# Attention scores on the keys that count: 256 neighbours and 128 of the residue class, in plain fp32 on 64x32 pieces

## The chip, the cores and the metric

The kernel runs on one core of one Trainium2 chip. The metric is the device time of one execution in microseconds; the kernel before takes 543.53 us as the median of three runs (543.14 to 543.93). The core has five engines that run their own instruction streams in order of program and meet through semaphores: TensorE (PE in the profile, with PEld for its weight loads), VectorE (DVE), ScalarE (ACT), GpSimd (POOL) and SyncE (SP, which here only issues transfers).

## The reference

One layer of an encoder for 512 positions of 1024 features, cut to the attention group:

```python
DILATED_PATTERNS = ((128, 1), (512, 4), (2048, 16))
for window, dil in DILATED_PATTERNS:
    half = window // (2 * dil)
    offs = jnp.arange(-half, half + 1) * dil          # 129 offsets, step dil
    bias = rel_bias[t5_bucket(offs)].T
...
for offs, bias in pats:                               # for each block of 128 queries
    kpos = pos[:, None] + offs[None, :]
    valid = (kpos >= 0) & (kpos < S)
    logits = einsum('bqhd,bqjhd->bhqj', qb, k[:, clip(kpos)]) * scale + bias
    logits = where(valid, logits, NEG_INF)
    lse = logsumexp(logits); p = exp(logits - lse)
    outs.append(einsum('bhqj,bqjhd->bqhd', p, v[:, clip(kpos)])); lses.append(lse)
o = sum(softmax(lses) * outs)                          # over the three patterns
```

There are 8 heads of 64 features. Combined by their softmax denominators, the three patterns are one softmax in which a key at distance `rel` counts as often as patterns contain it. All distances up to 64 occur; beyond 64 only multiples of 4 (up to 256) and of 16 do. Around the attention stand: an RMSNorm and one combined input projection (x_r, gate, q, k, v), a recurrent group (convolution, gates, a forward and a backward scan), an output projection of both groups (each after its own RMSNorm) with a residual, an MLP with squared ReLU, and a last RMSNorm.

## The kernel before, in words

Almost all matrix work is fp32 split into a rounded high part and a low part (`hi`, `lo`), three matmuls per product (`mm3`, L304 to L307). DVE and ACT make the two parts of the weights three chunks ahead (`conv_hi`, `conv_lo`), and SP streams the raw weights through three buffers (`wraw`).

The order on PE, ACT, DVE and POOL is that of the program, written by hand. The stages: input and x_r projection, V projection with the recurrent gates woven in (L669), gate projection (L708; the V accumulators are copied to `vs` in it), K and Q of head pair 0 (L909), six fillers (`PRE`, L986), and then the attention loop (L1004). The work splits into four head pairs p, two heads e = 0, 1 each.

The loop runs over i = 0 to 4 and u = 0 to 3. In step (i, u) it issues the scores of query tile u of pair i (`att_s`), the transposes for pair i - 1 (`att_t`), bias, row minimum and exp for pair i (`att_e`), and fillers. A filler is one eighth of a K or Q projection of a later pair, or after 48 of these one step of the output projection of the recurrent group. Between the two kinds the deque of fillers holds a `None`; the `fill` that meets it runs `load_x` first (L931): eight loads of x and four of `ws` on SP's queue, and on POOL's queue seven loads that add to `ws` in place. Their sums are needed by the attention half of the output projection. Each of the first four rounds has 16 fillers, the fifth five (`FILL`). `plan` hangs the splits of q and k and the recurrent group's leftovers on keys (i, u, place).

- `att_s`, L751: for each head a 128x512 score tile over all 512 keys, two fp32r matmuls: the stationary operand holds the high part of q in one half of the rows and its low part in the other, the moving operand the high part of k twice, then the low part twice. `s_hi` and `s_lo` make them, and SP copies each half of k to the other half of the rows.
- `att_e`, L759: DVE adds the bias (`tws`, a Toeplitz tile that SP reads from `nbd` with one element's shift per partition) and takes the row minimum; ACT takes the exp and its sum. Distances in no pattern have a bias that makes the exp zero.
- `att_t`, L777: four transposes of 128x128 per head and key tile into one PSUM bank of the tag `et`, and a copy by ACT.
- `att_z`, `att_r`: reciprocal of the sums, spread and transposed to rows (`prow`, L384).
- `att_av`, L854: V times the transposed exps, plain fp32, the two heads in the two column halves; pair 0 at (2, 0), pairs 1 and 2 at (4, 0), pair 3 behind the loop. Behind that come the column sums (`pcs`, L404), `rcol` by a power on POOL (L392), and the rest of the output projection and the MLP.

PSUM has eight banks in three tags: `pj` 4, `gs` 2, `et` 2. Score tiles use `gs`.

Of the kernel before, what the change touches and what calls it, by code (L numbers as in the profile page):

```python
# [17 lines left out]
P = 128  # L18
S = 512
# [52 lines left out]

def bias_onehot():
    rel = np.arange(-(S - 1), S)
# [12 lines left out]
    oh = np.zeros((NBUCK + 1, 2 * S), np.float32)  # L87
    oh[NBUCK, :] = NEG
    idx = np.arange(rel.size)
    keep = m > 0  # L90
# [11 lines left out]
def hybrid_kernel(ctx: ExitStack, tc, xw, xn, w_in, w_v, w_out, w_up, w_dn, gates, vecs, rel, onehot, fg, out):  # L102
# [318 lines left out]
    oht = [work.tile([NB3, S], FT, name="oht", tag="g", bufs=NG) for _ in range(2)]  # L421
    nbd = dram.tile([NH, 2 * S], FT, name="nbd")
# [5 lines left out]
    def bias_round(i):  # L428
        if i == 0:
            r = slice(NBUCK, 2 * NBUCK)  # L430
            nc.vector.tensor_copy(relr, relt)
            nc.vector.tensor_tensor(relr[r], relt[r], f(relr)[r], op=OP.subtract)
        t = work.tile([NB3, S], FR, name="ohr", tag="g", bufs=NG)
        ohr.append(t)
        r = slice(3 * NBUCK, NB3)
        nc.vector.tensor_copy(t, oht[i])
        nc.vector.tensor_tensor(t[r], oht[i][r], f(t)[r], op=OP.subtract)

    def bias_prep():
        for i in range(2):  # L440
            pbz = ps_("pbias", "pj")
            nc.tensor.matmul(pbz, lhsT=relr, rhs=ohr[i], start=True, stop=True)
            nbs = g_("nbs", shape=(NH, S))
            nc.vector.tensor_scalar(nbs, pbz[0:NH, :], -1.0, None, op0=OP.mult)
            nc.scalar.dma_start(nbd[:, i * S:(i + 1) * S], nbs)
# [3 lines left out]
    def load_tw(h):  # L449
        t = work.tile([P, 1024], FT, name="tw", tag="tw", bufs=4)[:, :896]  # L450
        ap = bass.AP(tensor=nbd.tensor, offset=nbd.offset + h * 2 * S, ap=[[1, P], [1, 896]])
        nc.sync.dma_start(t, ap)
        tws[h] = t
# [185 lines left out]
    for i in range(2):  # L639
        nc.gpsimd.dma_start(oht[i], onehot[:, i * S:(i + 1) * S])  # L640
# [58 lines left out]
    vs = big.tile([P, 4, S], FT, name="vs", tag="bigC")  # L699
# [8 lines left out]
    for n, th in enumerate(gsteps):  # L708
        th()
        lru_hooks(32 + n)  # L710
        if n in (19, 21, 27, 29):
            tt = {19: 0, 21: 2, 27: 3, 29: 1}[n]
            act(vs[:, tt, :], pv[tt], AF.Copy, scale=rcol[:, tt:tt + 1])
# [3 lines left out]

    def q_evac(p, pp):
        t = raw[p, 0] = g_("qraw")
        stt(t[:, ::-1], pp, -(DH ** -0.5), rstd, op0=OP.mult, op1=OP.mult)  # L720

    def k_evac(p, pp):
        t = raw[p, 1] = g_("kraw")
        nc.vector.tensor_tensor(t, pp, rstd, op=OP.mult)

    def s_hi(p, is_k, e):
        t = sp[p, is_k, "h", e] = g_("kh" if is_k else "qs", FR)
        own, other = halves[e], halves[1 - e]  # L730
        act(t[own], raw[p, is_k][own], AF.Copy)
        if is_k:
            nc.sync.dma_start(f(t)[other], f(t)[own])

    def s_lo(p, is_k, e):
        hi = sp[p, is_k, "h", e]
        own, other = halves[e], halves[1 - e]
        if is_k:
            t = sp[p, 1, "l", e] = g_("kl", FR)
            nc.vector.tensor_tensor(t[own], raw[p, 1][own], f(hi)[own], op=OP.subtract)  # L740
            nc.sync.dma_start(f(t)[other], f(t)[own])
        else:
            nc.vector.tensor_tensor(hi[other], raw[p, 0][own], f(hi)[own], op=OP.subtract)
        if e == 1:
            del raw[p, is_k]
# [3 lines left out]
    psq = {}  # L749

    def att_s(p, qt):  # L751
        c0 = P * qt
        psq[p] = [ps_("ps", "gs") for _ in range(2)]
        for e in range(2):
            q = sp[p, 0, "h", e][:, c0:c0 + P]
            nc.tensor.matmul(psq[p][e], lhsT=q, rhs=sp[p, 1, "h", e], start=True, stop=False)
            nc.tensor.matmul(psq[p][e], lhsT=q, rhs=sp[p, 1, "l", e], start=False, stop=True)  # L757

    def att_e(p, qt):  # L759
        if qt == 0:  # L760
            en[2 * p], en[2 * p + 1] = [], []
            zs[p] = small("zz", 8)
        pss = psq.pop(p)
        c0 = P * qt
        for e in range(2):
            h = 2 * p + e
            t = g_("e")
            mn = small("mn", 1)
            nc.vector.tensor_tensor_reduce(t, pss[e], tws[h][:, c0:c0 + S], 1.0, 3.0e38, OP.add, OP.min, mn)
            act(t, t, AF.Exp, scale=-1.0, bias=mn, accum_out=zs[p][:, 2 * qt + e:2 * qt + e + 1])  # L770
            en[h].append(t)
        if qt == 3:
            for e in range(2):
                del sp[p, 0, "h", e], sp[p, 1, "h", e], sp[p, 1, "l", e]
            del tws[2 * p], tws[2 * p + 1]

    def att_t(h, jt):  # L777
        pt = ps_("pt", "et")
        for qt in range(4):
            nc.tensor.transpose(pt[:, qt * P:(qt + 1) * P], en[h][qt][:, jt * P:(jt + 1) * P], ident)  # L780
        t = g_("ett")
        act(t, pt, AF.Copy)
        et[h, jt] = t
        if jt == 3:
            del en[h]

    pav, zrow, rzbs = {}, {}, {}
# [66 lines left out]
    def att_av(p, jts):  # L854
        if 0 in jts:
            pav[p] = ps_("pav", "gs" if p else "pj")
        for jt in jts:
            for e in range(2):
                a = slice(64 * e, 64 * e + 64)
                h = 2 * p + e  # L860
                nc.tensor.matmul(pav[p][a, :], lhsT=vs[:, jt, h * DH:(h + 1) * DH], rhs=et.pop((h, jt)),  # L861
                                 start=jt == 0, stop=jt == 3)
        if 3 in jts:
            y = g_("yp")
            nc.vector.tensor_tensor(y[:, ::-1], pav.pop(p), zrow.pop(p), op=OP.mult)
            y_sq(y, 1)
            at[p] = g_("at")
            act(at[p], y, AF.Copy, scale=vec("yg", 4 + p))
# [39 lines left out]
    KSPLIT = {7: s_hi, 8: s_lo}  # L908
    for n, th in enumerate(q_thunks(0, 1) + q_thunks(0, 0)):  # L909
        th()  # L910
        if n in KSPLIT:
            for e in range(2):
                KSPLIT[n](0, 1, e)
        if n % 4 == 0:
            lru_gelu(n // 4)
# [61 lines left out]
    for i in range(3):  # L977
        for key, (is_k, fn, e) in {(0, 2): (1, s_hi, 0), (0, 3): (1, s_hi, 1), (1, 0): (1, s_lo, 0), (1, 1): (1, s_lo, 1),
                                   (2, 2): (0, s_hi, 0), (2, 3): (0, s_hi, 1), (3, 0): (0, s_lo, 0), (3, 1): (0, s_lo, 1)}.items():
            plan.setdefault((i,) + key, []).append(lambda fn=fn, a=(i + 1, is_k, e): fn(*a))  # L980
# [5 lines left out]
    for n in range(PRE):  # L986
        if n == 0:
            for fn in (s_hi, s_lo):
                for e in range(2):
                    fn(0, 0, e)  # L990
        fill(1)
# [11 lines left out]
    AVS = {2: (0,), 4: (1, 2)}  # L1003
    for i in range(5):  # L1004
        for u in range(4):
            if i < 4:
                att_s(i, u)
                if u == 0 and i < 3:
                    load_tw(2 * i + 2)
                if u == 2 and i < 3:  # L1010
                    load_tw(2 * i + 3)
            if i >= 1:
                att_t(2 * i - 2, u)
                att_t(2 * i - 1, u)
            if i < 4:
                att_e(i, u)
            if u == 0 and i >= 1:
                att_z(i - 1)
            if u == 0:
                for p in AVS.get(i, ()):  # L1020
                    att_av(p, range(4))
# [6 lines left out]
            if u == 0:  # L1028
                for p in AVS.get(i, ()):
                    att_y(p)  # L1030
# [4 lines left out]
            beside(i, u, 4)  # L1035
    assert not plan
# [47 lines left out]
    att_av(3, range(4))  # L1084
# [570 lines left out]
```

## Time and profile before

| what | value |
| --- | --- |
| median of three runs | 543.53 us (543.14 to 543.93) |
| span of the profiled execution, first to last instruction | 542.3 us |
| PE busy | 533.9 us, 98% |
| DVE, ACT, POOL busy | 433.2, 363.2, 64.0 us |
| scores, 64 matmuls (L756, L757) | 97.6 to 169.2 us (starts) |
| transposes of exps, 128 (L780) | 113.5 to 187.2 us (starts) |
| V times exps, 32 calls, 64 records (L861) | 133.0 to 191.9 us (starts) |

The profiled execution is a single one, recorded by the hardware; its span is 1.2 us under the median, which also holds what lies before the first and behind the last instruction. A row of a timeline gives start and length in us, then engine, line, operation, output <- inputs, and what ended the engine's idle time before it. A matmul's length is modelled and overlaps its successor; the distance of two starts is what it costs. An fp32 matmul leaves two load records and two matmul records, an fp32r matmul one of each. "SPq" and "PEldq" are the sequencers of SP and PE: a row of SPq is the issue of a transfer, not its duration.

### The profile page before, as it was taken

The page shows a single profiled execution, that of the slowest core. Times are in us where ns is not written, and L with a number is a line of the kernel's source. Part 1 is how long each engine was busy: PE and PEld are TensorE (multiplying, and loading weights), DVE is VectorE, ACT ScalarE, POOL GpSimd, SP SyncE. Part 2 cuts the span into 40 slices and gives each one's busy share as a digit, 9 for nine tenths or more (in the row PEclk, how much of TensorE's full clock was granted, in tenths as well). Part 3 has the DMA queues.
Part 4 walks back from the last instruction along what each step waited for, and adds up shares of the span by engine and source line. Part 5 has one row for each costly group of instructions (what it writes and reads, how often), then busy time and mean ns, then how long its engine had stood idle before and what let it go on. Part 6 is the DMA issues. An engine that isn't in the chain of part 4 may idle for free.

```text
span 542.3 us, 8179 instructions
## 1 busy us (share of the span) xinstructions
PE 533.9 (98%) x3027; PEld 452.8 (83%) x3027; DVE 433.2 (80%) x631; ACT 363.2 (67%) x573; POOL 64.0 (12%) x91
## 2 busy tenths in 40 slices
PE   8999999999999999999999999999999999999995
PEld 7856888787887568899999888888999999888884
DVE  6897788997674688889769987869856887986985
ACT  7667973788774844767566855566566686755665
POOL 3330000000001031001030122001001020131000
PEclk9999999999999999999999999999999999999999
DMA  7655276454388788774677799994987496799804
GB/s 273 221 171 142 53 249 180 131 178 140 89 333 224 173 147 205 255 254 131 187 162 184 197 234 277 274 365 120 289 230 204 140 202 181 182 291 256 209 1 157
DMA packets 34360, 106.96 MB, mean 197 GB/s; under 512 B 4228, under 2 KB 5124, under 8 KB 34320
## 3 DMA queue, kind: packets, MB, share of 16 engines
q1 hardware_dynamic: 26032, 77.41, 41.9%
q0 software_dynamic: 7968, 28.76, 28.5%
q8 instruction: 24, 0.39, 0.3%
q10 hardware_dynamic: 320, 0.26, 0.2%
q14 instruction: 16, 0.13, 0.1%
HBM read 98.00 MB, written 4.23 MB: 188 GB/s over the span
## 4 chain that ended last, share of the span: by engine, by line
PE 84%; DVE 6%; ACT 4%; DMA 3%; issue 1%; ACTq 0%; SPq 0%; DVEq 0%
PE pu L305 10%; PE pu L306 10%; PE pu L307 10%; PE pd L307 9%; PE pd L305 9%; PE pd L306 9%; PE pav L861 3%; PE pt L780 2%; PE pqk L305 2%; PE pqk L307 2%; PE pqk L306 2%; PE pwo L305 2%; PE pwo L307 2%; PE pwo L306 2%; DVE wlo L261 2%; PE ps L757 1%
## 5 line engine op out<-in xcount | busy, mean ns | idle before, releaser
L261 DVE TENSOR_TENSOR wlo<-wraw,whi 128x1024 fp32r<-128x1024 f32 x73 | 88.9, 1221 | 21.6 <-ACT whi L253 21.4
L253 ACT ACTIVATE whi<-wraw 128x1024 fp32r<-128x1024 f32 x70 | 74.1, 1060 | 39.3 <-PE pd L307 19.3
L306 PE MATMUL pd<-wlo,ah 128*128 128x512 f32 (+1 forms) x195 | 75.2, 386 | 0.0
L305 PE MATMUL pd<-whi,ah 128*128 128x512 f32 (+1 forms) x195 | 75.2, 386 | 0.0
L307 PE MATMUL pd<-whi,al 128*128 128x512 f32 (+1 forms) x195 | 75.2, 386 | 0.0
L306 PE MATMUL pu<-hl,whi 128*128 128x256 f32 x224 | 63.4, 283 | 0.0
L307 PE MATMUL pu<-hh,wlo 128*128 128x256 f32 x224 | 63.4, 283 | 0.0
L305 PE MATMUL pu<-hh,whi 128*128 128x256 f32 x224 | 63.4, 283 | 0.0
L253 ACT ACTIVATE whi<-tw 128x1024 fp32r<-128x1024 f32 x36 | 38.0, 1060 | 35.2 <-PE pu L306 10.0
L305 PE MATMUL pu<-h2h,whi 128*128 128x256 f32 (+1 forms) x200 | 60.2, 301 | 0.3 <-ACT hm L1078 0.3
L306 PE MATMUL pu<-h2l,whi 128*128 128x256 f32 (+1 forms) x200 | 60.0, 300 | 0.0
L307 PE MATMUL pu<-h2h,wlo 128*128 128x256 f32 (+1 forms) x200 | 60.0, 300 | 0.0
L261 DVE TENSOR_TENSOR wlo<-tw,whi 128x1024 fp32r<-128x1024 f32 x36 | 44.0, 1223 | 16.5 <-ACT whi L253 16.5
L305 PEld LDWEIGHTS pu<-hh,whi 128*128 128x128 f32 x224 | 43.0, 192 | 0.0
L306 PEld LDWEIGHTS pu<-hl,whi 128*128 128x128 f32 x224 | 43.0, 192 | 0.0
L307 PEld LDWEIGHTS pu<-hh,wlo 128*128 128x128 f32 x224 | 43.0, 192 | 0.0
L253 ACT ACTIVATE whi<-ts 128x1024 fp32r<-128x1024 f32 x24 | 25.5, 1061 | 25.9 <-PE pd L307 18.1
L307 PEld LDWEIGHTS pd<-whi,al 128*128 128x128 f32 x195 | 36.6, 188 | 7.4
L306 PEld LDWEIGHTS pd<-wlo,ah 128*128 128x128 f32 x195 | 36.6, 188 | 7.4
L305 PEld LDWEIGHTS pd<-whi,ah 128*128 128x128 f32 x195 | 36.6, 188 | 7.3
L305 PEld LDWEIGHTS pu<-h2h,whi 128*128 128x128 f32 x200 | 38.3, 191 | 2.0 <-ACT hm L1078 0.8
L307 PEld LDWEIGHTS pu<-h2h,wlo 128*128 128x128 f32 x200 | 38.3, 191 | 1.3
(265 smaller groups left out, 1262.3 us busy)
## 6 DMA issues: line engine op xcount, KB each, us to landing
wraw<-in_w_up_dram SPq DMA_DIRECT2D x25, 512.0 KB, 3.9
ts<-in_w_dn_dram POOLq DMA_DIRECT2D x24, 512.0 KB, 13.6
wraw<-in_w_dn_dram SPq DMA_DIRECT2D x24, 512.0 KB, 8.9
tw<-in_w_up_dram SPq DMA_DIRECT2D x15, 512.0 KB, 10.1
tw<-in_w_up_dram POOLq DMA_DIRECT2D x15, 512.0 KB, 7.6
wraw<-in_w_in_dram SPq DMA_DIRECT2D x13, 512.0 KB, 3.5
ts<-in_w_dn_dram SPq DMA_DIRECT2D x8, 512.0 KB, 4.8
tw<-in_w_dn_dram SPq DMA_DIRECT2D x8, 512.0 KB, 8.0
```

What stands on the lines that cost most here:

```text
L253: act(hi, raws[i], AF.Copy)
L261: nc.vector.tensor_tensor(lo, r, f(splits[i][0]), op=OP.subtract)
L305: nc.tensor.matmul(o, lhsT=a[0], rhs=b[0], start=bool(first), stop=False, skip_group_check=on)
L306: nc.tensor.matmul(o, lhsT=a[0], rhs=b[1], start=False, stop=False, skip_group_check=on)
L307: nc.tensor.matmul(o, lhsT=a[1], rhs=b[0], start=False, stop=bool(last), skip_group_check=on)
L757: nc.tensor.matmul(psq[p][e], lhsT=q, rhs=sp[p, 1, "l", e], start=False, stop=True)
L780: nc.tensor.transpose(pt[:, qt * P:(qt + 1) * P], en[h][qt][:, jt * P:(jt + 1) * P], ident)
L861: nc.tensor.matmul(pav[p][a, :], lhsT=vs[:, jt, h * DH:(h + 1) * DH], rhs=et.pop((h, jt)), start=jt == 0, stop=jt == 3)
```

## The change

Queries are taken in tiles u from the end of the sequence (tile u holds positions 511 - 128u downwards), within a tile sorted by residue class modulo 4, 32 queries per class. Scores are split in two kinds. *Near*: the up to 256 keys around a query tile, for distances up to 64. *Far*: the 128 keys of the query's own residue class, for distances over 64. The bias masks each distance in one of the two.

- `s_hi` and `s_lo` go, with their SP copies; the scores are plain fp32 matmuls of the q and k tiles themselves. A call has 64 rows (one head) and 32 columns (one class), so that 4 x 2 pieces cover the array. Per pair: 32 near calls over 192 or 256 keys and 32 far calls over 128. `att_s` runs at u = 0 (near tiles 0 and 1, all far tiles) and u = 2 (near tiles 2 and 3). Near scores use `gs`, far ones two `pj` banks per pair.
- `k_far` (ACT) makes a copy of k sorted by class.
- `att_f` (DVE) adds bias and takes the minimum of the far scores, two tiles at u = 0 and two at u = 1; for tiles 0 and 3 POOL also writes zeros to 64 columns of the exp tile that no scores cover. `att_e` does the near part, starting its minimum from the far one, and one exp over both.
- `att_t` has three bank-fulls of four blocks per head instead of four: "a", "b" and "c" (far). The "b" blocks of tiles 0 and 3 contain the zeroed columns.
- `att_av` runs for pair i - 1 at the end of step (i, 3), from a V shifted by 64 positions (`vs`, made by eight half-height copies on ACT) and a V by class (`vc`, made by five SP transfers in `v_far`).
- The bias has 384 near and 256 far columns; `load_tw` issues two transfers per head.

The core of the diff:

```diff
+    def v_evac(tt):
+        r = rcol[:, tt:tt + 1]
+        for a, j in ((0, tt), (1, (tt + 1) % 4)):
+            own, other = halves[a], halves[1 - a]
+            act(vs[other, j, :], pv[tt][own], AF.Copy, scale=r[own])
+
+    def v_far():
+        for j in range(4):
+            for a, b, s in (((0, P, 32 * j - 16),) if j else ((0, 64, 112), (64, P, 0))):
+                n = (b - a) // 4
+                nc.sync.dma_start(vc[s:s + n], vs[a:b, j, :])
...
-    def s_hi(p, is_k, e):
-    def s_lo(p, is_k, e):
...
+    def k_far(p):
+        t = raw[p, 2] = g_("kfar")
+        act(t.rearrange("p (c s) -> p s c", c=4), raw[p, 1].rearrange("p (s c) -> p s c", c=4), AF.Copy)
...
+    def att_s(p, u0):
+        if u0 == 0:
+            pfar[p] = [ps_("pf", "pj") for _ in range(2)]
+        pnear[p] = [ps_("pn", "gs") for _ in range(2)]
+        for u in (u0, u0 + 1):
+            k0, k1 = keys(u)
+            o = (u - u0) * 2 * P + k0 - (320 - P * u)
+            for c in range(4):
+                r = slice(32 * c, 32 * c + 32)
+                for e in range(2):
+                    q = raw[p, 0][halves[e], u * P + 32 * c:u * P + 32 * c + 32]
+                    nc.tensor.matmul(pnear[p][e][r, o:o + k1 - k0], lhsT=q, rhs=raw[p, 1][halves[e], k0:k1],
+                                     start=u == u0, stop=True, skip_group_check=True)
+        for u in range(4) if u0 == 0 else ():
+            for c in range(4):
+                r = slice(32 * c, 32 * c + 32)
+                for e in range(2):
+                    q = raw[p, 0][halves[e], u * P + 32 * c:u * P + 32 * c + 32]
+                    nc.tensor.matmul(pfar[p][e][r, u * P:(u + 1) * P], lhsT=q, rhs=raw[p, 2][halves[e], (3 - c) * P:(4 - c) * P],
+                                     start=u == 0, stop=True, skip_group_check=True)
+    def att_f(p, u):
...
+        for e in range(2):
+            t = g_("e")
+            m = mf[2 * p + e, u] = small("mf", 1)
+            c = 2 * P if u == 3 else 0
+            nc.vector.tensor_tensor_reduce(t[:, c:c + P], pfar[p][e][:, u * P:(u + 1) * P], tws[2 * p + e][1][:, 32 * u:32 * u + P],
+                                           1.0, 3.0e38, OP.add, OP.min, m)
+            if u in (0, 3):
+                g = slice(5 * 64, 6 * 64) if u == 0 else slice(0, 64)
+                nc.gpsimd.memset(t[:, g], 0.0)
...
+            nc.vector.tensor_tensor_reduce(t[:, o + a:o + a + n], pnear[p][e][:, b:b + n], tws[h][0][:, a:a + n],
+                                           1.0, mf.pop((h, u)), OP.add, OP.min, mn)
+            v = t[:, 64:3 * P] if u == 3 else t[:, :P + a + n]
+            act(v, v, AF.Exp, scale=-1.0, bias=mn, accum_out=zs[p][:, 2 * u + e:2 * u + e + 1])
...
+    BLOCKS = {"a": ((0, 0), (1, 1), (1, 0), (2, 1)), "b": ((2, 0), (3, 1), (0, 1), (3, 0)), "c": ((0, 2), (1, 2), (2, 2), (3, 2))}
+
+    def att_t(h, x):
         pt = ps_("pt", "et")
+        for i, (u, b) in enumerate(BLOCKS[x]):
+            c = (2 if u == 3 else 0) if b == 2 else b + (u != 3)
+            nc.tensor.transpose(pt[:, i * P:(i + 1) * P], en[h][u][:, c * P:(c + 1) * P], ident)
...
+    def att_av(p):
+        pav = ps_("pav", "et")
...
+        for c in range(4):                     # far: 128 columns each
+            av(pick, vc[:, 3 - c, :], "c", pick, c == 0, False)
+        for j, x, c in ((3, "a", 0), (2, "a", 1), (1, "b", 0)):
+            av(lambda t: t[:, (3 - j) * P:(5 - j) * P], vs[:, j, :], x, lambda t: t[:, c * 2 * P:(c + 1) * 2 * P], False, False)
+        av(lambda t: cols4(t, 0, (3 * P, 2), (1, P)), vs[:, 0, :], "b", lambda t: t[:, 2 * P:], False, True)
...
     for i in range(5):
         for u in range(4):
+            if i < 4 and u in (0, 2):
+                att_s(i, u)
+                if i < 3:
+                    load_tw(2 * i + 2 + u // 2)
+            if i >= 1 and u < 3:
+                att_t(2 * i - 2, "abc"[u])
+                att_t(2 * i - 1, "abc"[u])
             if i < 4:
+                if u < 2:
+                    att_f(i, 2 * u)
+                    att_f(i, 2 * u + 1)
                 att_e(i, u)
...
             beside(i, u, 4)
+            if u == 3 and 1 <= i < 4:
+                att_av(i - 1)
```

More of the change, by code (lines that the diff above doesn't have):

```diff
@@ L69, in up_quadrants @@
     w[f:f + 4] = a.reshape(4, P, 2 * S).copy()
+NEAR = 64
+NW = 3 * P
+CW = 2 * P
 def bias_onehot():
-    rel = np.arange(-(S - 1), S)
+    near = np.arange(NW) - (NW // 2 - 1)
+    far = 4 * (np.arange(CW) - (P - 1))
+    rel = np.concatenate([near, far])
     m = np.zeros(rel.shape, np.int64)
@@ L420, in hybrid_kernel @@
     relt = consts.tile([NB3, P], FT, name="relt")
-    oht = [work.tile([NB3, S], FT, name="oht", tag="g", bufs=NG) for _ in range(2)]
-    nbd = dram.tile([NH, 2 * S], FT, name="nbd")
+    BCOL = (slice(0, NW), slice(NW, NW + CW))
+    oht = [work.tile([NB3, S], FT, name="oht", tag="g", bufs=NG)[:, :n] for n in (NW, CW)]
+    nbd = dram.tile([NH, NW + CW], FT, name="nbd")
     ohr = []
@@ L440, in bias_prep @@
         for i in range(2):
+            n = (NW, CW)[i]
             pbz = ps_("pbias", "pj")
[L442 removed]
+            nc.tensor.matmul(pbz[:, :n], lhsT=relr, rhs=ohr[i], start=True, stop=True)
             nbs = g_("nbs", shape=(NH, S))
[L444 to L445 removed]
+            nc.vector.tensor_scalar(nbs[:, :n], pbz[0:NH, :n], -1.0, None, op0=OP.mult)
+            nc.scalar.dma_start(nbd[:, BCOL[i]], nbs[:, :n])
     tws = {}
     def load_tw(h):
[L450 to L453, printed above, removed]
+        t = work.tile([P, 1024], FT, name="tw", tag="tw", bufs=4)
+        o = nbd.offset + h * (NW + CW)
+        near, far = t[:, :2 * P], t[:, 2 * P:2 * P + 7 * 32]
+        nc.sync.dma_start(near, bass.AP(tensor=nbd.tensor, offset=o, ap=[[1, 4], [4, 32], [1, 2 * P]]))
+        nc.sync.dma_start(far, bass.AP(tensor=nbd.tensor, offset=o + NW, ap=[[0, 4], [1, 32], [1, 7 * 32]]))
+        tws[h] = (near, far)
     halves = (slice(0, 64), slice(64, 128))
@@ L747, in hybrid_kernel @@
-    et, en, zs = {}, {}, {}
[L749 to L760, printed above, removed]
+        stt(t, pp, -(DH ** -0.5), rstd, op0=OP.mult, op1=OP.mult)
@@ L1027, in hybrid_kernel @@
                 att_r(i - 1)
-            if u == 0:
-                for p in AVS.get(i, ()):
-                    att_y(p)
+            if u == 0 and i >= 2:
+                att_y(i - 2)
             beside(i, u, 2)
```

136 lines of the change are left out of this document (57 added, 79 removed).

## The prediction

> **What bounds the kernel now.** I read the page's head first, then a table of stretches, then the timeline of TensorE (PE) through the attention loop, and last the timelines of the two queues the change touches, GpSimd (POOL) and SyncE (SP).
>
> ```profile
> span 542.3 us, 8179 instructions
> PE 533.9 (98%) x3027; PEld 452.8 (83%) x3027; DVE 433.2 (80%) x631; ACT 363.2 (67%) x573; POOL 64.0 (12%) x91
> core 0: us, PE busy (x) PEld busy (x) DVE busy (x) ACT busy (x) POOL busy (x), PEclk, DMA share, GB/s
> 97.40:112.20 14.80, 14.70 (x65) 11.83 (x64) 14.35 (x29) 12.24 (x25) 0.00 (x0) 1.00 0.46 129
> 112.20:148.10 35.90, 35.90 (x196) 28.37 (x194) 27.39 (x57) 29.23 (x60) 1.05 (x1) 1.00 0.46 132
> 148.10:181.85 33.75, 33.75 (x177) 24.63 (x175) 17.02 (x37) 20.57 (x44) 3.68 (x4) 1.00 0.87 269
> 181.85:194.70 12.85, 12.70 (x69) 8.15 (x67) 11.14 (x23) 9.60 (x20) 2.66 (x3) 1.00 0.54 88
> 194.70:542.30 347.60, 340.88 (x2081) 305.95 (x2080) 284.13 (x375) 222.25 (x326) 42.47 (x48) 1.00 0.77 207
> ```
>
> From 97.4 to 194.7 us, the attention loop and its tail, PE never rests, while DVE and ACT have slack. So PE time saved there counts, if nothing else becomes late. The cut at 148.10 is the end of the last q projection, the one at 181.85 the transposes of (i, u) = (4, 1), the one at 194.70 the column sums (`pcs`). The second queue to look at is POOL's, idle on average but in order:
>
> ```profile
> 139.49 1.05 POOL L392 TENSOR_TENSOR rcol<-rv,mhalf 128x4 f32<-128x4 f32 x1 [107.49 <-DVE rv L389]
> 160.85 0.99 POOL L942 DMA_DIRECT2D ws<-in_w_out_dram  x1 [20.31 <-PE pt L780]
> 169.55 2.69 POOL L942 DMA_DIRECT2D ws<-in_w_out_dram  x3 [7.71 <-DMA ws<-in_w_out_dram]
> 185.58 0.88 POOL L942 DMA_DIRECT2D ws<-in_w_out_dram  x1 [13.34 <-DMA ws<-in_w_out_dram]
> 191.45 1.78 POOL L942 DMA_DIRECT2D ws<-in_w_out_dram  x2 [4.99 <-DMA ws<-in_w_out_dram]
> 196.04 1.14 POOL L392 TENSOR_TENSOR rcol<-rv,mhalf 128x4 f32<-128x4 f32 x1 [2.81 <-DVE rv L389]
> 148.74 4.36 SPq L936 DMA_DIRECT2D x<-in_xn_dram  x8
> 153.14 2.38 SPq L940 DMA_DIRECT2D ws<-in_w_out_dram  x4
> ```
>
> `load_x` puts seven accumulating loads into POOL's queue; three of them wait for an earlier one to land, and POOL is through with them only at 191.45 + 1.78 = 193.2 us. They follow the order of the program (L392, L942, L392). Before the change nothing urgent stood behind them.
>
> **The change, part by part.** Scores first.
>
> ```profile
> 168.50 0.39 PE L756 MATMUL ps<-kh,qs 128*128 128x512 f32 x1
> 168.73 0.39 PE L757 MATMUL ps<-kl,qs 128*128 128x512 f32 x1
> 169.42 1.04 PE L780 MATMUL pt<-ident,e 128*128 128x128 f32 x8
> 170.21 0.47 PE L305 MATMUL pwo<-whi,yh 128*128 128x512 f32 x1
> 170.99 0.40 PE L305 MATMUL pwo<-whi,yh 128*128 128x512 f32 x1
> 171.68 0.40 PE L305 MATMUL pwo<-whi,yh 128*128 128x512 f32 x1
> ...
> 181.85 1.04 PE L780 MATMUL pt<-ident,e 128*128 128x128 f32 x8
> 182.64 0.48 PE L305 MATMUL pwo<-whi,yh 128*128 128x512 f32 x1
> 183.73 0.66 PE L384 MATMUL prow<-ident,rzb 128*128 128x128 f32 x4
> 184.14 0.47 PE L305 MATMUL pwo<-whi,yh 128*128 128x512 f32 x1
> ...
> 31.47 2.37 PE L491 MATMUL pg<-xc,gwr 64*64 64x512 f32 x16
> 188.84 3.65 PE L861 MATMUL pav<-ett,vs 128*64 128x512 f32 x16
> 192.43 0.50 PE L305 MATMUL pwo<-whi,yh 128*128 128x512 f32 x1
> L305 PEldq EVENT_SEMAPHORE  x2: 51/51/51, 217.6 to 217.7; - x2
> ```
>
> Starts 0.23 us apart: 16 score matmuls of a head pair take 3.7 us now. Afterwards a pair has 64 fp32 calls, each two records (8 calls of `pav` leave 16), so 128 load-and-multiply steps. Two limits. Array: `pav` takes 3.59 us for 8 calls of 512 columns, two column tiles at once: four calls in a row, 0.9 us each with entry and exit, 0.86 without. `pg` puts 8 calls into about 2.3 us, so its 64x64 quadrants ran nearly four at a time. If 64x32 pieces run eight at a time, a pair's 896 near and 512 far columns take 1408/512 x 0.86 = 2.4 us; if only four at a time, 4.7. Issue: the last row is an answer for 217.55 to 217.68 us; two waits of PE's sequencer started in those 0.13 us, and the program has three loads and three matmuls between them. Less the wait's own 51 ns that is some 13 ns an instruction, 26 a step: 128 x 0.026 = 3.3 us. The slowest reading comes from the transposes: eight steps in 0.79 us (169.42 to 170.21), under 100 ns a step, 12.8 us a pair. I take 3.3, the direct reading, plus two entries and exits of about 0.3 us (3.65 - 4 x 0.86 = 0.2 for `pav`, rounded up): 3.9 against 3.7, a loss of 0.2 a pair, 0.8 over four.
>
> Transposes go from eight blocks of four to six per pair: 32 fewer at 0.79/8 = 0.1 us, a gain of 3.2 us. P x V goes per head from 2048 columns to 4 x 128 + 4 x 256 = 1536: 3.59 becomes 2.7 + 0.2, a gain of 0.7 a pair, 2.8 in all (its 32 steps need 0.8 us of issue, so issue doesn't bind). Net PE work: about -5.2 us.
>
> ```profile
> L769 DVE CUSTOM_DVE_ANT_0 e<-ps,tw 128x512 f32<-128x512 f32 x32 | 20.8, 687 | 7.4 <-PE ps L757 7.3
> L769 DVE DVE_READ_ACCUMULATOR2_ANT mn<- 128x1 f32 x32 | 2.7, 83 | 0.0
> L824 DVE TENSOR_TENSOR ol<-osum,oh 128x256 fp32r<-128x256 f32 x8 | 3.2, 415 | 0.0
> L743 DVE TENSOR_TENSOR qs<-qraw,qs 64x512 fp32r<-64x512 f32 x8 | 5.5, 687 | 0.9 <-ACT qs L731 0.7
> L757 PEld LDWEIGHTS ps<-kl,qs 128*128 128x128 f32 x32 | 6.0, 188 | 1.8 <-DMA kl<-kl 0.5
> L782 ACT ACTIVATE ett<-pt 128x512 f32<-128x512 f32 x32 | 17.3, 591 | 10.5 <-PE pt L780 9.3 <-issue 1.1
> tw<-nbd SPq DMA_DIRECT2D x8, 448.0 KB, 4.0
> ```
>
> DVE: 687 ns at 512 columns and 415 at 256 give 143 fixed and 1.06 a column, an estimate; 8 far (279) and 8 near (347 to 415) with 16 read-outs of 83 make 6.6 us a pair against 6.2, but four splits of 0.69 go. ACT loses four splits and two `ett` copies of 591 ns a pair, shortens its exps and gains one `k_far` (0.6, or twice that for its strided output). Both engines get lighter; PE covers them. In the first round DVE may hold the second `att_s` up for some 0.7 us (`pnear` has two buffers, and two far tiles stand ahead of the near one), which the dropped wait for `kl` (0.5) nearly repays. Four more V copies on ACT and five SP loads of `v_far` lie in the gate stage, a loop round ahead of their first reader, P x V of pair 0; 16 SP swaps of K go; `load_tw` issues two smaller transfers instead of one, most of a round before `att_e` reads them. All zero under that cover; without it each costs a transfer, up to the 4.0 us of the last row.
>
> **The zeros.** `att_f` adds `memset` on POOL for u = 0 and u = 3: columns that the "b" transposes read. For pairs 0 to 2 POOL is idle or ahead. Counted in fillers (6 before the loop, four a step), the `None` that runs `load_x` comes up at (2, 2), and pair 3's memsets are written at (3, 0) and (3, 1): behind all seven L942. Their reader is `att_t(6, "b")` at (4, 1).
>
> When does PE get there? Up to the end of the last q projection the old and new sums differ by: scores 11 steps of 0.92 against three pairs of 3.9, seven transpose pairs of 0.79 against six, one P x V of 3.6 against 2.9: 19.2 against 19.3. So `load_x` stays at 148.1 us and the L942 chain ends at 193.2. A filler takes 0.69 us (170.99 to 171.68), `prow` 0.4 (183.73 to 184.14). From 148.1 PE has 6 and then 16 fillers, P x V of pairs 1 and 2 (5.8), pair 3's scores (3.9), four transpose pairs (3.2), `prow` and one more filler: 29.2 us, so it stands before the "b" blocks at 177.3 and waits 16 us. The first three memsets then cost about 0.15 us each, an estimate from 0.20 for twice the columns:
>
> ```profile
> 0.73 0.20 POOL masks.py:197 MEMSET ident<- 128x128 f32 x1 [0.29 <-POOLq L1644]
> 1.04 3.79 PE L147 MATMUL pwarm<-ones 128*128 128x128 f32 x16 [1.04 <-DVE epsb L138]
> PEclk9999999999999999999999999999999999999999
> ```
>
> The transposes start at 193.7 instead of 181.85, +11.85; behind them one transpose pair (0.8) and 0.7 of the last P x V have gone: +10.3. From 194.7 on PE is the bound again, so the delay stays. After an idle start PE is slow: sixteen 128-column steps took 3.79 us, 0.24 each against 0.1 for the transposes. A restart after 16 us may cost the same, 16 x 0.13 = 2.1, or nothing; I take 2.0, since this is the only restart in the trace. Sum: 542.3 + 10.3 + 2.0 = 554.6. The profiled span lies 1.2 under the median of 543.53, so 555.8 as a median.
>
> By the Trainium skill, TensorE: Matmul & The Clock Gate, "What's actually happening", an idle window of about 3.4 us halves PE's clock for at least one such window; half of 3.4 is 1.7 us by that rule. The clock row above shows no such dip even in its first slice, the matmuls do; by the row alone the sum would be 553.8.
>
> **The rivals.** *Issue is slow or the pieces overlap less.* The same rows allow it: at 25 ns an instruction, 50 a step, a pair's scores take 6.4 + 0.6, 3.1 more; 2.6 pairs lie before `load_x`, so the whole chain moves 8 us: 564. At the 100 ns bound it is 580. Against it: the 13 ns row. The same skill page ("Wait — 56ns, not 53.3ns?") gives 62 ns a matmul where its sequencer decodes in software; by that rule 128 x 0.062 = 7.9 a pair, near this case.
>
> *The zeros hold DVE too.* If a near score tile must wait for the memset of the same tile, DVE stops at (3, 0) and PE at (3, 2), some 13 us of PE work earlier: 569. Against it: L942's first accumulate started at 160.85, before the last of SP's loads into the other slices of `ws` can have landed, so regions seem to be tracked.
>
> *Faster: pair 3's zeros are written before PE needs them.* If POOL's waits don't hold the memsets, or the loads finish early, the 5.2 us of PE come out: 538.3. It decides where the chain ends before about 182: 11 us sooner. Against it: one accumulate alone took 5.9 us (185.58 to 191.45), three took 16; even if the first took 5.9 instead of 8.7 the chain ends at 190, and PE still waits 13 us. `rcol` at 196.04 stands in the same queue, so with the chain where it is only 2.8 us could be won even without memsets: 540.7.
>
> **How the numbers follow.** Waiting behind the loads as summed: 0.70, 550 to 561 (chain end 190 to 197, restart 0 to 2.1). Slow issue: 0.12, 564. DVE held: 0.06, 569. Faster: 0.09, 538 to 541. No net effect: 0.03. Slower 0.88, same 0.03, faster 0.09, where 0.2%, about 1.1 us, is what a measurement tells from no change. For 8 in 10 the range runs from 547 to 566: the main case whole, most of slow issue, and a chain a few us shorter.
>
> **What would show it.** Right: POOL's memsets of pair 3 right after the last L942 near 193 us; PE idle for 12 to 18 us before an L780 transpose near 177, released by POOL; score steps about 26 ns apart; 96 transposes. Wrong: those memsets before 177, or a score stage of 6 us a pair, or a DVE that waits for POOL.

## The result, and the profile after

The changed kernel takes 553.12 us (median of four runs, 549.62 to 554.31) against 543.69 (543.14 to 543.93) for the kernel before on the same chip: a ratio of 1.016, 95% interval 1.013 to 1.020. 555.8 had been predicted. The profiled run took 554.31 us, the slowest of the four, with a span of 552.5, 10.2 more than before. The head of its page, with the row of TensorE's granted clock, comes first.

```profile
span 552.5 us, 9169 instructions
PE 530.6 (96%) x3507; PEld 452.7 (82%) x3507; DVE 423.9 (77%) x679; ACT 352.9 (64%) x557; POOL 65.7 (12%) x107
PEclk9999999999999689999999999999999999999998
```

PE has 3.3 us less work than before and ends 10.2 us later; the clock row has a dip that it didn't have. The view of waits gives the three longest of PE behind the gate stage (engine, line, what it waited for: us in all, times, longest):

```profile
PE pt L833 <- POOL e L803: 8.7, 1, 8.7
PE pn L779 <- DVE mn L818: 2.2, 1, 2.2
PE pcs L411 <- DVE ysq L588: 1.3, 1, 1.3
```

The first is the predicted one. The timeline of POOL shows its queue around it:

```profile
153.31 0.99 POOL L1005 DMA_DIRECT2D ws<-in_w_out_dram  x1 [10.23 <-DMA ws<-in_w_out_dram]
...
180.64 0.87 POOL L1005 DMA_DIRECT2D ws<-in_w_out_dram  x1 [13.62 <-DMA ws<-in_w_out_dram]
186.52 1.77 POOL L1005 DMA_DIRECT2D ws<-in_w_out_dram  x2 [5.00 <-DMA ws<-in_w_out_dram]
187.61 1.10 POOL L803 MEMSET e<- 128x64 f32 x4
204.23 1.14 POOL L399 TENSOR_TENSOR rcol<-rv,mhalf 128x4 f32<-128x4 f32 x1 [15.51 <-DVE rv L396]
```

The four zero fills of pair 3 run directly behind the last accumulating load, as foretold. The chain of loads began at 153.31, not at 160.85 as before: its first load waits for a transfer of `ws`, and SP issues that one ahead of the eight of x, where it stood behind them before.

```profile
149.49 0.33 SPq L1003 DMA_DIRECT2D ws<-in_w_out_dram  x1
149.91 3.91 SPq L999 DMA_DIRECT2D x<-in_xn_dram  x8
```

PE's timeline has the transposes that read the zeros:

```profile
179.41 0.44 PE L833 MATMUL pt<-ident,e 128*128 128x128 f32 x2 [0.47 <-ACT ett L835]
188.51 1.54 PE L833 MATMUL pt<-ident,e 128*128 128x128 f32 x6 [8.66 <-POOL e L803]
189.70 0.78 PE L312 MATMUL pwo<-whi,yh 128*128 128x512 f32 x1
190.28 0.63 PE L313 MATMUL pwo<-wlo,yh 128*128 128x512 f32 x1
190.70 0.63 PE L314 MATMUL pwo<-whi,yl 128*128 128x512 f32 x1
...
202.71 1.23 PE L411 MATMUL pcs<-ones,ysq 128*128 128x1 f32 x8 [1.33 <-DVE ysq L588]
```

Behind the wait the starts of the filler's matmuls are 0.42 us apart (190.28 to 190.70) where they were 0.23. The table of stretches says why, in its column PEclk: 0.84 of full speed over the 14 us behind the wait.

```profile
core 0: us, PE busy (x) PEld busy (x) DVE busy (x) ACT busy (x) POOL busy (x), PEclk, DMA share, GB/s
179.40:188.51 9.11, 0.44 (x3) 0.20 (x3) 1.06 (x3) 0.44 (x1) 2.86 (x7) 0.70 0.50 100
188.51:202.71 14.20, 12.87 (x75) 9.89 (x75) 9.01 (x16) 7.73 (x16) 0.20 (x3) 0.84 0.38 72
202.71:552.50 349.79, 342.38 (x2080) 307.31 (x2080) 284.41 (x375) 222.66 (x326) 42.39 (x48) 0.99 0.75 203
```

The 10.2 us can be divided at two points that both traces have, the first "b" transposes held at (4, 1) and the column sums `pcs`:

| stretch | before | after | difference | predicted |
| --- | --- | --- | --- | --- |
| start to the held transposes | 181.85 | 188.51 | +6.7 | +11.85 |
| from there to `pcs` | 12.85 | 14.20 | +1.3 | -1.5 + 2.0 |
| `pcs` to the end | 347.60 | 349.79 | +2.2 | 0 |

The span came out only 2.1 us under the forecast (552.5 for 554.6) because 3.0 of the 5.2 us by which the first row is too high are covered by losses in the other two, which the forecast had at 0.5 and 0. That is in part luck. The experiments take these rows one by one.

### The profile page after: what moved, and what is told of

Its sections match the earlier page's. It is cut to its first block, busy times and chain, and to the rows that moved or that the text cites. A ratio compares the mean times of both kernels' runs of the same rounds, so it can differ in the third digit from the quotient of the medians.

```text
span 552.5 us, 9169 instructions
## 1 busy us (share of the span) xinstructions
PE 530.6 (96%) x3507; PEld 452.7 (82%) x3507; DVE 423.9 (77%) x679; ACT 352.9 (64%) x557; POOL 65.7 (12%) x107
## 4 chain that ended last, share of the span: by engine, by line
PE 85%; DMA 7%; DVE 4%; ACT 1%; issue 1%; POOL 1%; SPq 0%; DVEq 0%; POOLq 0%; ACTq 0%
PE pu L314 10%; PE pu L312 10%; PE pu L313 10%; PE pd L314 9%; PE pd L312 9%; PE pd L313 9%; DMA ws<-in_w_out_dram 6%; PE pqk L312 3%; PE pqk L313 2%; PE pqk L314 2%; PE pg L502 2%; PE pv L312 1%; PE pt L833 1%; PE pv L314 1%; PE pv L313 1%; PE pp L314 1%
```

## The experiments

Each kernel was timed beside the kernel before (543.6 to 543.9 in the three groups). Line numbers are those of the changed kernel; where an edit removes or adds lines, they move a little.

**The zeros off POOL.**

```diff
-                nc.gpsimd.memset(t[:, g], 0.0)
+                (nc.vector if p == 3 else nc.gpsimd).memset(t[:, g], 0.0)
```

> Pair 3's four zero fills (e, columns that the "b" transposes read) are written by DVE instead of POOL; everything else as in the changed kernel. Theory A (the zeros queue behind POOL's accumulating loads and PE waits for them): the 8.7 us wait of PE before the transposes of (4, 1) goes, and with it the half clock behind the restart (about 2 us) and perhaps the 2.2 us that the span lost behind the column sums: 553.1 - 8.7 - 2 = 542.4, at best 540. That is below the kernel before (543.7) by up to 0.6%. Theory B (the stage became longer for other reasons, and the wait for POOL only coincides with a wait for ett or DVE): the wait is renamed, and the time stays within 2 us of 553. Either way DVE gets four fills of about 0.15 us, under PE's cover.

Measured: 540.58 us (539.21 to 545.39, ten runs), ratio 0.996 (0.993 to 0.999). The wait is gone, not renamed: the transposes go through but for the 0.5 us of `ett`, which the changed kernel had too, and `pcs` starts at 189.20, 5.5 us earlier than in the kernel before.

```profile
PE pcs L411 <- DVE ysq L588: 1.3, 1, 1.3
PE pn L779 <- DVE mn L818: 1.3, 1, 1.3
PE pt L833 <- DVE rz L844: 0.6, 1, 0.6
```

The place of four fills of 0.15 us thus made the difference between 1.6% slower and 0.4% faster than before. Theory A holds, and its rival, that the stage as such had become slower, falls.

**The zeros ahead in POOL's queue.** Another way to the same end: the fills stay on POOL, the seven accumulating loads are collected in `load_x` and issued behind them.

```diff
-                nc.gpsimd.dma_start(t, oblock(b), accum_op=OP.add)
+                later.append((t, b))
...
+            if (i, u) == (3, 1):
+                for t, b in later:
+                    nc.gpsimd.dma_start(t, oblock(b), accum_op=OP.add)
```

> The zeros stay on POOL; its seven accumulating loads of w_out are issued behind pair 3's zeros (after the minima of (3, 1)) instead of with the loads of x. Theory A (the order in POOL's queue is the whole cause): the 8.7 us wait of PE for the zeros goes, but the chain of loads, 35 us from its first accumulate to its last (153.3 to 188.3), starts about 168 instead of 153 and ends about 203; rcol, which the x of the out projection needs at about 190, stands behind it, so about 10 us are lost there instead: 548 to 555, no better than the changed kernel. Theory B (the loads are slow only because they run beside other transfers): the chain takes under 25 us at its new place and the time falls to 542 to 545.

Measured: 543.25 us (538.58 to 544.24, ten runs), ratio 0.997 (0.994 to 0.999). PE's wait for POOL is gone, and no loss came in its place, so the 548 to 555 of theory A were wrong; the time lies in the range of theory B, but not for its reason, as POOL's timeline shows:

```profile
140.13 0.31 POOL L803 MEMSET e<- 128x64 f32 x3
142.26 0.15 POOL L803 MEMSET e<- 128x64 f32 x1 [1.83 <-PE prow L391]
145.33 0.24 POOL L803 MEMSET e<- 128x64 f32 x2 [2.92 <-PE pt L833]
150.83 0.99 POOL L1078 DMA_DIRECT2D ws<-in_w_out_dram  x1 [5.26 <-DMA ws<-in_w_out_dram]
...
183.17 1.78 POOL L1078 DMA_DIRECT2D ws<-in_w_out_dram  x2 [5.05 <-DMA ws<-in_w_out_dram]
```

I had put the loads at the time when PE works on (3, 1), about 168 us. But POOL doesn't wait for PE's place in the program: the fills need only free `e` buffers, which the transposes of an earlier pair give back, so they were done at 145.6 and the loads began at 150.83, when their data was there. The chain takes 34 us, where the changed kernel took 35, so theory B's reason is wrong. The cause is the order in POOL's queue. Whether this order has a price can't be read from runs that spread from 538.6 to 544.2 us; the last experiment below shows it.

**PE kept busy through the wait.**

```diff
+            if i == 4 and u == 1:
+                pd = ps_("pdummy", "gs")
+                for _ in range(34):
+                    nc.tensor.matmul(pd[:, :P], lhsT=ones, rhs=ones, start=True, stop=True)
```

> The changed kernel with 34 matmuls of ones by ones (128 columns, into a PSUM tile that nobody reads) put ahead of PE's "a" transposes of (4, 1), so that PE works while POOL's zeros are late. The output is the reference's. Theory A (part of the loss is the half clock behind an idle PE): PE shows no dip of its clock at the restart, and 2 to 3 us come back: 550 to 551. Theory B (the clock dip costs nothing net, since the stage waits for DVE or ACT anyway): 553 as it was. If the 34 matmuls take longer than the wait, it is slower by the excess, which the trace would show as a wait for POOL of nearly zero.

Measured: 548.75 us (547.83 to 549.32), ratio 1.009 (1.007 to 1.010). With the useless work the kernel is 4.4 us faster (548.75 for 553.12), more than the 2 to 3 foretold. In the profiled run:

```profile
177.26 7.75 PE L1069 MATMUL pdummy<-ones 128*128 128x128 f32 x68
...
186.39 0.94 PE L833 MATMUL pt<-ident,e 128*128 128x128 f32 x6 [1.17 <-POOL e L803]
187.09 0.47 PE L312 MATMUL pwo<-whi,yh 128*128 128x512 f32 x1
...
198.45 1.05 PE L411 MATMUL pcs<-ones,ysq 128*128 128x1 f32 x8 [1.35 <-DVE ysq L588]
```

From the held transposes to `pcs` it takes 12.06 us (186.39 to 198.45) instead of 14.20: the half clock behind the 8.7 us wait cost 2.1 us, and the prediction had 2.0. The two profiled spans differ by 6.0 us. The remainder lies at two other places, where this run, with the same waits, shows full clock and the changed kernel's profile didn't: at (0, 2) and behind `pcs` (348.05 us from there to the end instead of 349.79). The first of these stands ahead of the added matmuls, so they can't have brought it; only the 2.1 us are shown to be theirs.

**DVE's order in the first round.** The changed kernel's timeline around (0, 2), where the forecast had put 0.7 us:

```profile
104.60 0.39 PE L314 MATMUL pqk<-h_hi,wlo 128*128 128x512 f32 x1
107.20 1.98 PE L779 MATMUL pn<-kraw,qraw 64*32 64x256 f32 x32 [2.21 <-DVE mn L818]
109.11 0.79 PE L312 MATMUL pqk<-h_hi,whi 128*128 128x512 f32 x1
```

DVE has the steps `ga`, `gt` (L570, L571) of two recurrent tiles, 4 x 0.69 us, between the first near minima and those that free `pnear`. Two theories stood: this order, or the raw weight that came late because the transfers of `v_far` share its queue. ACT waited for that weight, and DVE for ACT:

```profile
98.72 1.06 ACT L260 ACTIVATE whi<-wraw 128x1024 fp32r<-128x1024 f32 x1 [3.85 <-DMA wraw<-in_w_in_dram]
```

```diff
-    plan = {(0, 0, 0): [end(0)], (0, 0, 2): [sq_(0), add], (0, 0, 3): [end(1)],
-            (0, 1, 1): [sq_(1)],
-            (0, 2, 3): [add],
+    plan = {(0, 1, 0): [end(0)], (0, 1, 2): [sq_(0), add], (0, 1, 3): [end(1)],
+            (0, 2, 1): [sq_(1)],
+            (0, 3, 1): [add],
```

> The changed kernel with DVE's extra work of the first round (two normalising steps, two squarings and an addition) put one to four slots later in the hand-written order, behind the near scores of (0, 2). Theory A (PE waits 2.2 us for DVE at (0, 2) because these steps stand ahead of the near score of (0, 0) and (0, 1), and then runs at 0.64 clock): that wait goes, about 4 us earlier at the last q projection; the load chain of x and w_out is issued behind that projection, so POOL's zeros and the whole stage move with it: 549. Theory B (that wait is made by the late raw weight, for which ACT waited 3.85 us at 98.7): the wait stays above 1.5 us and the time stays at 553.

Measured: 550.53 us (550.42 to 551.38), ratio 1.013 (1.011 to 1.015). PE's wait there is gone although ACT still waited 3.64 us for the weight, and the scores begin 2.5 us earlier. The only wait left of the near scores, 0.2 us for q, is that of (0, 0):

```profile
104.72 1.39 PE L779 MATMUL pn<-kraw,qraw 64*32 64x256 f32 x32
...
PE pn L779 <- DVE qraw L751: 0.2, 1, 0.2
98.89 1.06 ACT L260 ACTIVATE whi<-wraw 128x1024 fp32r<-128x1024 f32 x1 [3.64 <-DMA wraw<-in_w_in_dram]
```

The late weight alone doesn't hold PE; with DVE's steps in their first order it does count, as the profiles of the kernels with that order show. Where ACT waited 3.7 to 3.9 us for the weight, PE waited 2.2 to 3.0 at (0, 2); where ACT waited 2.4 to 2.8 (the zeros on DVE, the moved loads, and the next run), PE waited 1.1 to 1.3. So the wait comes of both delays together, and the later order takes it away whichever way the weight comes. Of the 4 us expected 2.6 came between the medians, 3.9 between the two profiled spans.

```diff
-    v_far()
...
+            if (i, u) == (0, 1):
+                v_far()
```

> The changed kernel with the five transfers that put V together by residue class issued at (0, 1) of the loop, instead of behind the gates on the queue that also brings the raw weights. Theory A (these transfers make the raw weight late for ACT, and so DVE late at (0, 2)): ACT's wait of 3.85 us for the weight goes, and with it the wait of PE at (0, 2): 549 to 551. Theory B (the order of DVE's steps makes it): ACT's wait goes, PE's wait stays over 1.5 us and the time at 553. If the transfers now make a weight late in the loop, it shows as a wait of ACT for wraw between 105 and 125 us, and nothing is won.

Measured: 552.25 us (550.12 to 553.98), ratio 1.015 (1.012 to 1.018): inconclusive. SP's order isn't the one written, only the other engines' is, and the edit moved one transfer: the five issues stand at 80.03, 85.83 (two), 89.56 and 97.00 us, where the changed kernel has 79.47, 85.46 (two), 89.22 and 90.54. ACT still waits 2.44 us for the weight, and PE 1.3 at (0, 2), no less than in kernels without this edit. What these transfers cost wasn't settled.

**The price of strided operands.** The DVE operations that permute q and y became dearer, a cost that the forecast has no term for. They write with a stride; the experiment lets them read with one and write in a row. Behind its edit stand the groups (busy us, mean ns) of the kernel before, of the changed kernel and of this one.

```diff
-        o = cols4(t, S - 1, (-P, 4), (-1, 32), (-32, 4))
-        v = [x.rearrange("p (u a c) -> p u a c", u=4, a=32) for x in (pp, rstd)]
+        o = cols4(t, S - 1, (-P, 4), (-32, 4), (-1, 32))
+        v = [x.rearrange("p (u a c) -> p u c a", u=4, a=32) for x in (pp, rstd)]
...
-        o = cols4(y, S - 1, (-P, 4), (-1, 4), (-4, 32))
-        v = [x.rearrange("p (u c a) -> p u c a", u=4, c=4) for x in (pav, zrow.pop(p))]
+        o = cols4(y, S - 1, (-P, 4), (-4, 32), (-1, 4))
+        v = [x.rearrange("p (u c a) -> p u a c", u=4, c=4) for x in (pav, zrow.pop(p))]
```

> The changed kernel with the permutation of q and of y done on the read side: the two DVE operations read PSUM and the row scale strided and write 4 or 128 neighbours in a row (reversed), instead of reading in order and writing 128 or 16 bytes apart. Theory A (it is the strided write that makes them 1.10 to 1.13 us instead of 0.69): both fall to about 0.70 for q and, with runs of four, 0.7 to 1.1 for y; the wait of the column sums for DVE falls by up to 0.4, and the time by 0.4 to 2. Theory B (a stride on either side costs the same): 1.1 us stay, and 553.

```profile
L720 DVE SCALAR_TENSOR_TENSOR qraw<-pqk,rrow 128x512 f32<-128x512 f32 x4 | 2.8, 689 | 2.0 <-PE pqk L307 2.0
L865 DVE TENSOR_TENSOR yp<-pav,zrow 128x512 f32<-128x512 f32 x4 | 2.8, 692 | 9.5 <-PE pav L861 9.5
```

```profile
L751 DVE TENSOR_TENSOR qraw<-pqk,rrow 128x512 f32<-128x512 f32 x4 | 4.5, 1132 | 4.4 <-PE pqk L314 4.4
L930 DVE TENSOR_TENSOR yp<-pav,zrow 128x512 f32<-128x512 f32 x4 | 4.4, 1103 | 8.0 <-PE pav L914 8.0
```

```profile
L751 DVE TENSOR_TENSOR qraw<-pqk,rrow 128x512 f32<-128x512 f32 x4 | 4.3, 1086 | 4.7 <-PE pqk L314 4.7
L930 DVE TENSOR_TENSOR yp<-pav,zrow 128x512 f32<-128x512 f32 x4 | 4.3, 1072 | 8.0 <-PE pav L914 8.0
```

Measured: 552.92 us (549.56 to 553.97), ratio 1.015 (1.012 to 1.018). Theory B: on whichever side the stride lies, 512 fp32 elements take 1.07 to 1.13 us instead of the 0.69 of the kernel before, where q was written in reverse order but without a stride. By the Trainium skill, SBUF — State Buffer, "Door 1: The DMA port swizzle", SBUF works in lines of 16 bytes, four fp32, and PSUM in lines of 8, and an access that crosses to another line pays for it. This trace agrees in kind: every one of these forms leaves the line at nearly each element on one side, and takes 1.6 times as long. That the line is what sets the price isn't shown: no stride short of a line was run.

**What a score step costs.** PE's timeline of the changed kernel at (1, 0), then of one whose far pieces take 64 keys:

```profile
135.63 0.99 PE L779 MATMUL pn<-kraw,qraw 64*32 64x192 f32 x32
136.41 1.13 PE L786 MATMUL pf<-kfar,qraw 64*32 64x128 f32 x64
137.47 0.77 PE L833 MATMUL pt<-ident,e 128*128 128x128 f32 x5
```

```diff
-                    ... pfar[p][e][r, u * P:(u + 1) * P] ... raw[p, 2][halves[e], (3 - c) * P:(4 - c) * P],
+                    ... pfar[p][e][r, u * P:u * P + 64] ... raw[p, 2][halves[e], (3 - c) * P:(3 - c) * P + 64],
```

> The changed kernel with the far score pieces working 64 keys each instead of 128 (DVE reads the 64 scores twice, so it does as much as before; the scores of the other keys are left out). It measures one term: the 64 load-and-multiply steps of a pair's far scores take 1.09 us in the changed kernel (98.16 to 99.25). Theory A (the issue of the instructions sets it, 17 ns a step): 1.0 to 1.1 us stay with half the columns. Theory B (the array sets it, eight pieces abreast, 512 columns at 0.86 us): about 0.5 to 0.65 us. The time of the whole would fall by at most 4 x 0.5 = 2 us, less than this stage's waits spread.

```profile
136.21 0.90 PE L786 MATMUL pf<-kfar,qraw 64*32 64x64 f32 x64
137.04 1.09 PE L833 MATMUL pt<-ident,e 128*128 128x128 f32 x8
```

Measured: 553.6 us in one run, which says nothing; the rows do. 64 steps take 1.06 us (16.6 ns each) with 128 columns and 0.83 us (13 ns) with 64. Neither theory: half the columns save a fifth. 13 ns a step is an upper bound of what the issue needs, half of the 26 that the prediction took; what the rest of the 16.6 is wasn't separated.

**All repairs together.** The zeros on DVE, the later order and the later `v_far`:

> Pair 3's zeros on DVE, the later order of DVE's extra steps and the later transfers of V by class together. If the three causes add, PE shows neither the wait of 8.7 us nor that of 2.2 (1.3 with the zeros on DVE alone) at (0, 2): 540.6 - 1.3 = 539.3, with up to 2 us more if a dip of the clock goes too: 537.5 to 539.3. If the waits only hide each other (PE now waits for the raw weight or for ett instead): 540.6.

Measured: 538.52 us (537.84 to 539.15), ratio 0.990 (0.988 to 0.991), in the range for causes that add. The wait at (0, 2) is no longer in the list; the gain over the zeros alone is 2.1 us. That leaves the end of the attention, where `yp`, now 1.10 us, stands behind two splits on DVE:

```diff
-                    ..., ((4, 3, 4), [(o_lo, "s1", 0), (o_hi, "22", 0), (o_lo, "22", 0)])):
+                    ..., ((4, 3, 4), [(o_hi, "22", 0)])):
...
     att_av(3)
+    o_lo("s1", 0)
     att_y(3)
-    fill(3)
+    o_lo("22", 0)
+    fill(4)
```

> As the three causes together, and at the end of the attention: DVE's two splits of (4, 3, 4) stand behind the scaled output of the last pair (yp) instead of ahead of it, and four instead of three fillers stand ahead of the column sums. Theory A (behind the last P x V, DVE's queue and the 0.41 us that yp now takes more set the end, and PE's short waits there bring the clock down): the wait of 1.3 us for ysq shrinks below 0.5, no dip of the clock follows, and 1.5 to 2.5 us come out against the kernel without this edit: 535.5 to 537.5. Theory B (behind the column sums another wait takes its place, on rcol or x): under 0.7 us come out.

Measured: 536.14 us (535.95 to 536.31), ratio 0.985 (0.984 to 0.987), as theory A had it. The wait for `ysq` is gone; how much of that is the order and how much the filler more ahead of it wasn't separated. PE's longest wait from the attention on is now 0.6 us, and the clock row is flat:

```profile
PE pwo L312 <- DVE x L1121: 0.6, 2, 0.4
PE pt L832 <- DVE rz L843: 0.6, 1, 0.6
PE pt L832 <- ACT ett L834: 0.5, 1, 0.5
```

```profile
PEclk9999999999999999999999999999999999999999
```

The same with the zeros ahead in POOL's queue instead of on DVE:

> As the version with the tail mended, but the zeros stay on POOL and stand ahead of its accumulating loads, as in the run that moved the loads, instead of being written by DVE. Theory A (POOL's zeros cost nothing once no waiting instruction stands ahead of them): 536.1 as with DVE, or 0.2 to 0.6 less, for DVE's four fills; no wait of PE for POOL. Theory B (the loads come later by their place in the program, and their last reader waits): PE waits for the weights of the out projection around 186, and the time is 537 to 540.

Measured: 536.26 us (535.95 to 536.69), ratio 0.987 (0.986 to 0.989): no difference between the two places, so POOL's fills cost nothing there either. These two versions beat both kernels. The change is worth about 1.4% with these repairs. That the kernel before would gain nothing by the later orders is argued, not run: behind its first matmuls its longest wait of PE is 0.4 us.

## Why the prediction was right, step by step

The mechanism, the sign and the range were right: pair 3's zeros behind the chain of loads, PE idle before the "b" transposes, half clock at the restart. The two kernels that take the zeros out of that place show it. The terms of the sum were less good than their total: the chain's end, the length of the wait and the time of a score step all lie outside what the forecast named for its main case (190 to 197 us, 12 to 18 us, about 26 ns), and that the total still fell into its 550 to 561 is partly luck.

- *"The L942 chain ends at 193.2", "at 177.3 and waits 16 us".* 188.3 and 179.4 were measured, and 8.7 us. The chain began at 153.31 instead of 160.85, since SP here issues one `ws` load ahead of the eight of x; the forecast had carried its place over from the kernel before. That the range took in a shorter chain was right. PE came 2.1 us later than summed: the last q projection ended at 149.5 instead of 148.1, for the reason of the third point, and two waits of 0.60 and 0.47 us (for `rz` and `ett`) stand just ahead of the transposes.
- *"3.9 against 3.7, a loss of 0.2 a pair".* The near half-round takes 0.78 and 0.92 us (0.92 in the second half, 166.16 to 167.08), the far scores 1.06: 2.8 us a pair, a gain of 0.9. The step that failed is the choice of the issue limit, 3.3 us with "26 a step" from two semaphore waits, over the array's 2.4. The far pieces took 16.6 ns a step, and 13 with half the columns. The near half-rounds come close to the array's reading of eight pieces abreast: 448/512 x 0.86 = 0.75 us by the forecast's own rows, 0.78 and 0.92 measured. Slow issue, the rival, moved this term the wrong way.
- *"DVE may hold the second `att_s` up for some 0.7 us", "nearly" repaid.* It held PE up for 2.2 us and brought the clock down behind it. The count left out the four steps of 0.69 us that `plan` hangs between, and the raw weight that came late. The run with the later order shows the first: 2.6 us of the total. What the dearer q adds here wasn't run.
- *P x V and transposes, "a gain of 0.7 a pair" and 3.2.* 173.58 to 176.33 is 2.75 us against 3.59, a gain of 0.84; 96 transposes remain. Right.
- *The restart, "I take 2.0".* 2.1. Right, at this place.
- *"The delay stays" behind `pcs`, at no further cost.* 2.2 us more. Of these 1.6 to 1.7 (349.8 against 348.1) go with a dip of the clock behind the wait of 1.3 us for `ysq`; the other 0.5 (348.1 against 347.6) is there without a dip too, and what makes it wasn't looked for. The wait itself is part of the row above. The forecast had no price for strided writes on DVE (it had one for ACT's `k_far`, 1.12 us measured) and didn't look at what stands between P x V and the column sums.
- *Net PE work, -5.2.* With every wait repaired `pcs` starts at 186.97 with one filler more ahead of it: 194.70 - 186.97 + 0.69 = 8.4 us, in place of 5.2. The rival "faster" had the right content with a price too small: 538.3 for what became 536.1 with every repair. That the zeros on DVE alone gave 540.6, near its 540.7, is chance: those 540.7 were for a `rcol` held behind the loads, and there `rcol` ran at 190.54, 4.7 us after POOL was through with them.

## What to carry to other kernels

Four operations of 0.15 us can cost 10 us when they go into a queue behind instructions that wait for transfers: read the timeline of the queue that gets them, not the engine's busy share, and put them ahead of the loads, since a queue reaches it when its inputs are free and not when the program's other engines pass that line. On a kernel whose TensorE is 98% busy, count a wait at more than its length: what follows may run at half clock, and two small waits can cost much of what a change saves: with the zeros on DVE and the waits at (0, 2) and `pcs` left the kernel took 540.6 us, with those mended too 536.1. Go through every place where the changed stage hands over to DVE with the new durations, strided ones above all.

## What the runs showed of the hardware that was not expected

The same wait can cost its length or its length and 1.6 us more. The wait of 1.3 us before `pcs` is in nine of the profiled kernels, with the same instructions behind it. In six of them (the changed one, and those of the zeros, the order, the later `v_far`, the moved loads and the 64 keys) the clock falls to half for some 3.6 us (with the zeros on DVE, from 190.9 to 194.5 by the distance of the starts); in three (the kept-busy one, the repairs together, the read-side permutation) it doesn't. From `pcs` to the end it is 349.7 to 349.8 us in all six where a dip follows, and 348.05 to 348.2 in the three where none does. The stretches of 8.00 us from 1.3 us ahead of `pcs` (busy time of PE, granted clock, DMA share, GB/s), for the kernel with the zeros on DVE and the one with the repairs together:

```profile
187.90:195.90 8.00, 6.70 (x26) 0.79 0.81 145
```

```profile
186.72:194.72 8.00, 6.60 (x31) 1.00 0.67 121
```

This goes with the spread of the runs: 539.2 to 545.4 us with the zeros alone, 535.95 to 536.31 where no wait is over 0.6 us. The mean granted clock of those ten runs falls as their time rises, from 0.997 in the fastest three to 0.990 or 0.991 in the slowest three; which waits they paid for more wasn't seen, since only one was profiled. In the changed kernel itself the clock fell behind 2.2 us at (0, 2), in the kept-busy one it didn't behind the same 2.2. By the Trainium skill, TensorE: Matmul & The Clock Gate, "What's actually happening", the gate looks at a window of about 3.4 us that runs free of the kernel; that the same wait is punished or not, and for about one such window, agrees. That a whole idle window of 3.4 us is needed doesn't: a wait of 1.3 us, with 0.9 us of one-column matmuls behind it, was followed by half clock six times. What decides between the two wasn't settled here.
